# New prices in the plan that orders a mixer's side work, and a sigmoid's product that waits for its sigmoid

## The chip, the cores and the metric

One core of one Trainium2 chip runs the whole program. The metric is the device time of an execution in microseconds (us), shown as the median of several runs; one further execution was recorded by the profiler.

## The reference, cut to what matters

One layer, for a prompt of 1024 positions and 8 samples of 4 positions (1056 columns). A mixer of three head groups, whose outputs are joined and multiplied with `w_out`, and then an MLP with squared ReLU. Each has an RMS norm before and after, with scales from a conditioning vector.

```python
z = h @ w_in
za, zq, zf, zi, zg, zc = split(z)
ya, v_rows = _chunk_gmlp(za, ...)
yb, S = _hgrn2(zq, zf, zi, zg, lb, gn_g, s0)
yc, buf = _conformer_conv(zc, ...)
x = x + gt1 * rmsnorm(concat([ya, yb, yc]) @ w_out)
x = x + gt2 * rmsnorm(square(relu(h2 @ w_up)) @ w_down)
```

The gMLP group is u times a masked product of position weights (128 by 128) with the layer-normalised v, both after a GELU. The recurrence has 8 heads of 64 by 64; chunk by chunk it carries a state S with decay, gives `o = q S + scores v`, normalises o per head and multiplies with `silu(zg)`. The convolution has 31 taps, a layer norm and `y * sigmoid(y)` behind it.

## The kernel before, in words

Everything is kept with features on the partitions and the 1056 columns along the free axis, in three chunks of 352 columns. A **block** is one product of a 1024 by 128 weight with the normalised input: three chunks, 8 slices of the inner dimension, and three matmuls for each slice (`hi*hi`, `lo*hi`, `hi*lo`, both operands being split into two fp32r parts), so 72 matmuls. The results (`pmt`, three banks) are emptied by ScalarE (ACT) and VectorE (DVE). Weights come by DMA as `raw` and are split there as well: ACT writes `whi`, DVE `wlo`.

The blocks of the mixer run in the order convolution 0 and 1, pair 0, gate 0, pair 1, gate 1, pair 2, pair 3, gate 2, gMLP (four blocks: two of v, two of u), gate 3. A pair of heads has three blocks (f, q, v), a gate one, whose product with its sigmoid is `gq`. Behind gate 3, `finish()` lets all side work run to its end, and the output product begins (line 1529; input groups in the order 6, 7, 2, 3, 4, 0, 1, 5, where 6 and 7 are the convolution's, 0 and 1 the gMLP's, and 5 is pair 3).

All other work is side work, written as generators that stand in queues of different rank: `turn` (turned copies of v and k by PE), `recur` (a pair's recurrence), `stage` (its scans and decays), `norm` and `last` (the head norm), `gmlp`, `conv`. Within and after each chunk's products the kernel calls `step(t)` (line 224), which lets the generators go on in order of rank for as long as credit is left on the engines. All engines work in the order in which the program writes, so this decides what stands behind what.

Two things steer it. Each instruction passes through `Metered` (line 85; the instruction itself is issued at line 113), which takes its price from `dve_price`, `ActPrice`, `pool_price` or `pe_price`, charges it to the engine's credit and enters it in a `Plan`, a clock for each engine. And `until(...)` (line 244) makes a generator yield as long as the plan's clock says that the tiles named are not done, or no bank is free. All prices are fixed numbers in the code.

Names that matter below. In a pair's recurrence (`recur`): scores `sc`, sums of states `us`, two scans over the states (DVE), two turned copies `sv` of them by ACT (tiles `vf` and `K` in the trace, 64x960), the output products `ob`, and for the samples `uss` and `os_`, with the state `s0t`. Then `head_norm`: means `gnps` on PE, square root on ACT, three reciprocals on DVE, and the products `k<-k,vf` and `k<-k,gq`. In `stage`: three scans `R` and one over the whole of f. In `conv_tail`: a scale by feature on ACT, the sigmoid on ACT and the product with it on DVE. In `gmlp`: the turned v (`gvt`), its statistics and normalisation on DVE, then `gmps` (four groups of eight matmuls) and `gmsp` on PE, with `gmt` and `gu` behind them on DVE. `split_y` writes the output product's operands `yh` (ACT) and `yl` (DVE).

Of the kernel before, what the change touches and what calls it, by code (L numbers as in the profile page):

```python
# [38 lines left out]
class Plan:  # L39


    def __init__(self):
        self.free = dict.fromkeys(("pe", "act", "dve", "pool", "dma"), 0.0)
        self.done, self.used, self.banks = {}, {}, []
        self.moved = False
# [39 lines left out]
class Metered:  # L85
# [5 lines left out]
    def __getattr__(self, op):  # L91
        f = getattr(self._eng, op)
        if op == "memset":
            return f

        def call(**kw):
            out = kw["out"]
            n = 1
            for x in out.shape[1:]:
                n *= x  # L100
            ins = [x for k, x in kw.items() if k != "out" and hasattr(x, "tensor")]
            if op == "dma_start":
                if self._key == "pool":
                    self._plan.given("pool", 0.9, out, ins, 8.0)
                else:
                    self._plan.given("dma", out.shape[0] * n * 4 / 3e5, out, ins, 2.0)
                return f(**kw)
            price = self._price(op, n, kw)
            self._credit[self._key] -= price
            if self._key == "pe" and op == "matmul" and kw["lhsT"].dtype == F32R:  # L110
                price = n * 0.443e-3 + 0.005
            self._plan.given(self._key, price, out, ins)
            return f(**kw)  # L113

        return call


def dve_price(op, n, kw):
    if op == "reciprocal":
        return 0.1 + n * 6.25e-3  # L120
    if op in ("tensor_scalar", "tensor_copy"):
        return 0.07 + n * 0.55e-3
    if n <= 64:
        return 0.3
    return 0.11 + n * (1.17e-3 if op == "scalar_tensor_tensor" else 1.04e-3)


class ActPrice:
# [3 lines left out]

    def __init__(self):
        self.table = 0

    def __call__(self, op, n, kw):
        t = self.TABLES.get(kw.get("func"), self.table)
        load = 1.3 if t != self.table else 0.0
        self.table = t
        return load + 0.1 + n * 0.83e-3  # L140


def pool_price(op, n, kw):
# [16 lines left out]
def trunk_kernel(ctx: ExitStack, tc: tile.TileContext, xT, cT, wada0, wada, vec, cst, msk, win, wout, wup,  # L160
                 wdn, s0, sconv, aw, aws, arows, yT, hgp, hgs, cvp, cvs, gvs):
    nc = tc.nc
    ctx.enter_context(tc.manual_schedule())
    credit = {"dve": 0.0, "act": 0.0, "pe": 0.0, "pool": 0.0}
    plan = Plan()
    PE = Metered(nc.tensor, pe_price, credit, "pe", plan)
    ACT = Metered(nc.scalar, ActPrice(), credit, "act", plan)
    DVE = Metered(nc.vector, dve_price, credit, "dve", plan)
    POOL = Metered(nc.gpsimd, pool_price, credit, "pool", plan)
    SP = Metered(nc.sync, None, credit, "dma", plan)  # L170
# [12 lines left out]
    def r(ap):  # L183
        return ap.bitcast(F32R)
# [12 lines left out]
    def e(name):  # L197

        while not room():
            step(T_GROUP / 2)  # L200
        held[0] += 1
        return full(name)
# [4 lines left out]
    def rs(name):  # L207
        return sp.tile([128, 512], F32, tag="rs", name=name)
# [35 lines left out]
    def until(*aps, banks=0):  # L244

        while not plan.ready(aps, banks):
            yield 0.2
# [67 lines left out]
    def split_next(later=False):  # L315
# [12 lines left out]
        else:  # L328
            pool = wpools[n_w[0] % len(wpools)]
            hi = pool.tile(shape, F32, tag="whi", name="whi")  # L330
            lo = pool.tile(shape, F32, tag="wlo", name="wlo")
        ACT.copy(out=r(hi), in_=raw)

# [74 lines left out]
    def ada_copy(first):  # L408
        b, ps = first
        sb = mp.tile([128, 128], F32, tag="adasb", name="adasb")  # L410
        ACT.copy(out=sb, in_=ps)
        return b, sb
# [10 lines left out]
    def ada(q):  # L423
# [20 lines left out]
        sb = e("adasb")  # L444
        ACT.copy(out=sb[:, 0:512], in_=ps)
        yield from until(sb, banks=1)
# [37 lines left out]
    def token_rms(ps):  # L484
        n = ps.shape[0]
        rt = sp.tile([128, 4], F32, tag="rt", name="rt", bufs=3)[0:n, :]
        ACT.activation(out=rt, in_=ps, func=AF.Sqrt, scale=1.0 / 1024, bias=eps[0:n])
        return rt
# [21 lines left out]
    def rstd_from(ps):  # L510
        t = rstd_tile("rstd")
        ACT.activation(out=t, in_=ps, func=AF.Sqrt, scale=1.0 / 1024, bias=eps)
        DVE.reciprocal(out=t, in_=t)
# [9 lines left out]
    def add_square(tot, src, m, eng):  # L523

        sq = tot if m == 0 else rs("sqb")[:, 0:tot.shape[1]]
        ACT.activation(out=sq, in_=src, func=AF.Square)
        while pending:
# [403 lines left out]
    def conv_tail():  # L931
        while not room(3):
            yield 2.0
        sq, hi, lo = [e("y6")], e("cvhi"), e("cvlo")
        for c in range(NCH):
            DVE.tensor_tensor(out=ch(sq[0], c), in0=ch(cva[0], c), in1=ch(cva[1], c), op=ALU.add)
        yield 4.0

        def halves():
            ACT.copy(out=r(hi), in_=sq[0])  # L940
            POOL.tensor_tensor(out=r(lo), in0=sq[0], in1=hi, op=ALU.subtract)

        halves()
        yield from until(hi, lo)
        for c in range(NCH):
            yield from until(banks=1)
            mu = pb.tile([128, CW], F32, tag="b", name="cmu")
            mean_of(mu, mean256, ch(hi, c), ch(lo, c))
            s2 = rs("sq2")[:, 0:CW]
            for j in range(2):  # L950
                DVE.tensor_tensor(out=ch(cva[j], c), in0=ch(cva[j], c), in1=mu, op=ALU.subtract)
                ACT.activation(out=s2 if j else ch(sq[0], c), in_=ch(cva[j], c), func=AF.Square)
            DVE.tensor_tensor(out=ch(sq[0], c), in0=ch(sq[0], c), in1=s2, op=ALU.add)
            yield
        yield 4.0
        halves()
        yield from until(hi, lo, banks=3)
        vv = [pb.tile([128, CW], F32, tag="b", name="cvv") for c in range(NCH)]
        for c in range(NCH):
            mean_of(vv[c], mean256, ch(hi, c), ch(lo, c))  # L960
        drop(2)
        sq.append(e("y7"))
        for c in range(NCH):
            ACT.activation(out=ch(sq[0], c), in_=vv[c], func=AF.Sqrt, bias=eps, scale=1.0)
        yield 2.0
        for c in range(NCH):
            sd = ch(sq[0], c)
            DVE.reciprocal(out=sd, in_=sd)
            yield
            for j in range(2):  # L970
                a = ch(cva[j], c)
                DVE.tensor_tensor(out=a, in0=a, in1=sd, op=ALU.mult)
            yield
        yield 2.0
        for j in range(2):
            z = cva[j]
            ACT.activation(out=z, in_=z, func=AF.Identity, scale=vc(V_LNG + j, 1), bias=vc(V_LNB + j, 1))
            yield
            ACT.activation(out=sq[j], in_=z, func=AF.Sigmoid)
            DVE.tensor_tensor(out=sq[j], in0=sq[j], in1=z, op=ALU.mult)  # L980
            ys[6 + j] = sq[j]
            y_done[6 + j] = NCH
            drop()
            yield
# [212 lines left out]
    def recur(p, st):  # L1197
# [73 lines left out]
        yield  # L1271
        for hh in range(2):
            o = 64 * hh
            ACT.copy(out=sv[hh][o:o + 64, 1:16], in_=S[o:o + 64, :, 0:15].rearrange("p d b -> p b d"))
        ACT.copy(out=hg_o[:, p, :], in_=S[:, :, 15])

# [11 lines left out]
        oo, sq, hi, lo = k2, vf, e("gnhi"), e("gnlo")  # L1288
# [19 lines left out]
        for hh in range(2):  # L1308
# [7 lines left out]
                           op=ALU.mult)  # L1316
# [781 lines left out]
```

## Time and profile before

| what | us |
| --- | --- |
| median of 3 runs | 1248.2 (1248.02 to 1248.28) |
| the profiled execution's own time | 1246.52 |
| its span in the trace | 1244.7 |
| TensorE (PE) busy | 1211.6 (97%) |
| VectorE (DVE) busy | 900.4 (72%) |
| ScalarE (ACT) busy | 532.9 (43%) |
| GpSimd (POOL) busy | 62.9 (5%) |

The mixer with its products takes about the first third of the span; the output product's first matmul starts at 405.22. An engine's busy time is what its instructions take, without its waits; PE's has modelled ends, so that rows overlap. In a timeline a bracket at the end of a row is the idle time of the engine just before it, and what ended it. Tile names are the program's, without their numbers, and L113 is the helper's line, common to nearly all instructions.

### The profile page before, as it was taken

Reading aid. Unit: us, or ns where it says so; the run is one execution under the profiler, and the core shown is the slowest. Engines: PE = TensorE matmul, PEld = TensorE weight load, DVE = VectorE, ACT = ScalarE, POOL = GpSimd, SP = SyncE. Lnnn points to the kernel's source line nnn. Section 1 sums busy time; section 2 is a strip of 40 time slices with the busy share of each in tenths; the row PEclk is TensorE's granted clock in tenths of the full one; section 3 lists DMA queues with packets and bytes.
Section 4 is the critical chain, followed back from the end, with each engine's and each line's share of the span. In section 5 each row is a group of like instructions: output and inputs, shape, how many; then the busy total and the mean of one; then the engine's idle time right before and its main releaser. Section 6 shows DMA issues by size and latency. Waiting matters only on the chain.

```text
span 1244.7 us, 20853 instructions
## 1 busy us (share of the span) xinstructions
PE 1211.6 (97%) x8614; PEld 1168.0 (94%) x8614; DVE 900.4 (72%) x1469; ACT 532.9 (43%) x989; POOL 62.9 (5%) x107
## 2 busy tenths in 40 slices
PE   9999999999899999999999999999999999999995
PEld 7888889999889999899999999999999999999994
DVE  5799989687658768767687667657666766765766
ACT  6513364575754756556423312322332331232543
POOL 1000020212010011010000000000000000000001
PEclk9999999999999999999999999999999999999998
DMA  9559411111111475343201211210211121121218
GB/s 366 172 223 279 163 37 53 44 43 43 56 43 40 135 212 136 127 127 119 79 24 51 69 34 35 68 44 24 69 51 35 52 68 34 35 68 35 110 18 212
DMA packets 48846, 113.22 MB, mean 91 GB/s; under 512 B 10336, under 2 KB 24832, under 8 KB 48624
## 3 DMA queue, kind: packets, MB, share of 16 engines
q1 hardware_dynamic: 44432, 99.22, 23.6%
q0 software_dynamic: 4320, 12.68, 4.4%
q8 instruction: 67, 1.10, 0.4%
q14 instruction: 27, 0.22, 0.1%
HBM read 101.75 MB, written 10.14 MB: 90 GB/s over the span
## 4 chain that ended last, share of the span: by engine, by line
PE 83%; DVE 8%; ACT 6%; issue 1%; DMA 1%; POOL 0%; ACTq 0%; DVEq 0%; POOLq 0%
PE pmt L113 75%; PE adaps L113 2%; PE stps L113 1%; DVE acc L113 1%; PE pmt L744 1%; DMA o<-in_xT 1%; DVE wlo L113 1%; ACT K L113 1%; ACT vf L113 1%; DVE q L113 1%; PE sc L113 1%; ACT whi L113 1%; PE ob L113 0%; DVE o L113 0%; DVE vf L113 0%
## 5 line engine op out<-in xcount | busy, mean ns | idle before, releaser
L113 PE MATMUL pmt<-ah,whi 128*128 128x352 f32 (+2 forms) x744 | 241.5, 325 | 1.1 <-ACT ah L113 0.6
L113 PE MATMUL pmt<-al,whi 128*128 128x352 f32 (+2 forms) x744 | 241.3, 324 | 1.0 <-DVE al L113 1.0
L113 PE MATMUL pmt<-ah,wlo 128*128 128x352 f32 (+2 forms) x744 | 240.2, 323 | 0.0
L113 DVE TENSOR_TENSOR acc<-acc,pmt 128x352 f32<-128x352 f32 (+1 forms) x320 | 157.1, 510 | 81.0 <-PE pmt L113 80.0
L113 DVE TENSOR_TENSOR wlo<-raw,whi 128x1024 fp32r<-128x1024 f32 (+2 forms) x113 | 134.5, 1193 | 46.1 <-ACT whi L113 46.1
L113 ACT CAST whi<-raw 128x1024 fp32r<-128x1024 f32 (+2 forms) x113 | 114.2, 1014 | 97.4 <-PE pmt L113 95.6
L113 PEld LDWEIGHTS pmt<-al,whi 128*128 128x128 f32 x744 | 139.9, 188 | 3.7 <-DVE al L113 1.5
L113 PEld LDWEIGHTS pmt<-ah,whi 128*128 128x128 f32 x744 | 139.7, 188 | 2.9 <-ACT ah L113 1.2
L113 PEld LDWEIGHTS pmt<-ah,wlo 128*128 128x128 f32 x744 | 139.8, 188 | 0.4
L113 ACT COPY acc<-pmt 128x352 f32<-128x352 f32 x63 | 28.3, 451 | 196.8 <-PE pmt L113 161.8
L113 PE MATMUL pmt<-h22hi,wlo 128*128 128x352 f32 x256 | 82.7, 323 | 0.0
L113 PE MATMUL pmt<-h22hi,whi 128*128 128x352 f32 x256 | 82.5, 322 | 0.0
L113 PE MATMUL pmt<-h22lo,whi 128*128 128x352 f32 x256 | 82.3, 322 | 0.0
L113 DVE SCALAR_TENSOR_TENSOR cva<-cvx,vec_t,cva 128x1024 f32<-128x1024 f32 x60 | 77.8, 1296 | 1.2
L113 PE MATMUL pmt<-s,whi 128*128 128x352 f32 x312 | 75.6, 324 | 0.0
L113 ACT ACTIVATE relu<-pmt 128x352 f32<-128x352 f32 x57 | 26.4, 463 | 102.4 <-PE pmt L113 102.4
L113 DVE TENSOR_TENSOR al<-rsq,ah 128x352 fp32r<-128x352 f32 x96 | 49.2, 523 | 14.1 <-ACT ah L113 8.0
L113 PE MATMUL pmt<-h1hi,whi 128*128 128x352 f32 x168 | 55.7, 332 | 2.6 <-DVE gq L113 2.6
L113 PE MATMUL pmt<-h0hi,whi 128*128 128x352 f32 x168 | 55.4, 330 | 0.8 <-DVE gq L113 0.8
L113 PE MATMUL pmt<-h2hi,whi 128*128 128x352 f32 x168 | 56.3, 335 | 0.0
L113 DVE TENSOR_TENSOR rsq<-relu 128x352 f32<-128x352 f32 x45 | 23.5, 523 | 43.0 <-ACT relu L113 41.8
L113 PEld LDWEIGHTS pmt<-s,whi 128*128 128x128 f32 x312 | 54.5, 188 | 0.0
(391 smaller groups left out, 2929.8 us busy)
## 6 DMA issues: line engine op xcount, KB each, us to landing
rawada<-in_wada SPq DMA_DIRECT2D x48, 512.0 KB, 8.4
raw<-in_wup SPq DMA_DIRECT2D x36, 512.0 KB, 3.5
raw<-in_wdn SPq DMA_DIRECT2D x48, 256.0 KB, 3.1
raw<-in_win SPq DMA_DIRECT2D x22, 512.0 KB, 3.6
raw<-in_wout SPq DMA_DIRECT2D x20, 512.0 KB, 3.5
raw<-in_wdn SPq DMA_DIRECT2D x12, 512.0 KB, 3.6
x<-in_xT SPq DMA_DIRECT2D x6, 528.0 KB, 6.4
o<-in_xT POOLq DMA_DIRECT2D x6, 528.0 KB, 7.4
```

Of the source, the lines that this page charges most:

```text
L113: return f(**kw)
L744: nc.tensor.matmul(out=pss[m, c], lhsT=r(w_first[m][i % 2][:, k, :]), rhs=r(h[c][i // 2][:, k, :]), start=k == i == 0, stop=k == 7 and i == 2)
```

## The change

Five edits, four of them to prices: a scan costs 0.05 + 2.2e-3 us per element in place of 0.11 + 1.04e-3; the two turned copies `sv` cost 1.75e-3 per element in place of 0.83e-3; each scale or bias that is given by feature adds 0.1 to an ACT instruction; fills (`memset`) are entered in the plan, where they had no price. The fifth is one line in `conv_tail`: the generator yields until the plan says that the sigmoid is done before it issues the sigmoid's product. The arithmetic is the same; what moves is the order.

```diff
@@ -91,7 +91,14 @@
     def __getattr__(self, op):
         f = getattr(self._eng, op)
         if op == "memset":
-            return f
+            def fill(out, value):
+                n = 1
+                for x in out.shape[1:]:
+                    n *= x
+                self._plan.given(self._key, 0.08 + n * 0.85e-3, out, ())
+                return f(out, value)
+
+            return fill
 
         def call(**kw):
             out = kw["out"]
@@ -118,6 +125,8 @@
 def dve_price(op, n, kw):
     if op == "reciprocal":
         return 0.1 + n * 6.25e-3
+    if op == "tensor_tensor_scan":
+        return 0.05 + n * 2.2e-3
     if op in ("tensor_scalar", "tensor_copy"):
         return 0.07 + n * 0.55e-3
     if n <= 64:
@@ -132,12 +141,16 @@
 
     def __init__(self):
         self.table = 0
+        self.turned = False
 
     def __call__(self, op, n, kw):
         t = self.TABLES.get(kw.get("func"), self.table)
         load = 1.3 if t != self.table else 0.0
         self.table = t
-        return load + 0.1 + n * 0.83e-3
+        by_feature = sum(not isinstance(kw.get(x, 0.0), float) for x in ("scale", "bias"))
+        each = 1.75e-3 if self.turned else 0.83e-3
+        self.turned = False
+        return load + 0.1 + n * each + 0.1 * by_feature
 
 
 def pool_price(op, n, kw):
@@ -164,7 +177,8 @@
     credit = {"dve": 0.0, "act": 0.0, "pe": 0.0, "pool": 0.0}
     plan = Plan()
     PE = Metered(nc.tensor, pe_price, credit, "pe", plan)
-    ACT = Metered(nc.scalar, ActPrice(), credit, "act", plan)
+    act_price = ActPrice()
+    ACT = Metered(nc.scalar, act_price, credit, "act", plan)
     DVE = Metered(nc.vector, dve_price, credit, "dve", plan)
     POOL = Metered(nc.gpsimd, pool_price, credit, "pool", plan)
     SP = Metered(nc.sync, None, credit, "dma", plan)
@@ -977,6 +991,7 @@
             ACT.activation(out=z, in_=z, func=AF.Identity, scale=vc(V_LNG + j, 1), bias=vc(V_LNB + j, 1))
             yield
             ACT.activation(out=sq[j], in_=z, func=AF.Sigmoid)
+            yield from until(sq[j])
             DVE.tensor_tensor(out=sq[j], in0=sq[j], in1=z, op=ALU.mult)
             ys[6 + j] = sq[j]
             y_done[6 + j] = NCH
@@ -1271,6 +1286,7 @@
         yield
         for hh in range(2):
             o = 64 * hh
+            act_price.turned = True
             ACT.copy(out=sv[hh][o:o + 64, 1:16], in_=S[o:o + 64, :, 0:15].rearrange("p d b -> p b d"))
         ACT.copy(out=hg_o[:, p, :], in_=S[:, :, 15])
 
```

How the order moves, at three places. First DVE at the end of the convolution, where the two products `y<-y,cva` (128x1056) take the sigmoid; `gq` empties a bank of PE, `QB` is a product of pair 2's `stage`. Before:

```order
L113 TENSOR_TENSOR wlo<-raw,whi 128x1024
L113 TENSOR_TENSOR cva_714<-cva_714,y_2387 128x352
L113 TENSOR_TENSOR cva_1289<-cva_1289,y_2387 128x352
L113 TENSOR_TENSOR gq<-pmt,sgg 128x352
L113 TENSOR_TENSOR y_2387<-y_2387,cva_714 128x1056
L113 TENSOR_TENSOR y_3029<-y_3029,cva_1289 128x1056
L113 TENSOR_TENSOR gq<-pmt,sgg 128x352
L113 TENSOR_TENSOR QB<-q,f 128x32x16
```

And now:

```order
L120 TENSOR_TENSOR cva_714<-cva_714,y_2407 128x352
L120 TENSOR_TENSOR cva_1301<-cva_1301,y_2407 128x352
L120 TENSOR_TENSOR gq<-pmt,sgg 128x352
L120 TENSOR_TENSOR y_2407<-y_2407,cva_714 128x1056
L120 TENSOR_TENSOR gq<-pmt,sgg 128x352
L120 TENSOR_TENSOR wlo<-raw,whi 128x1024
L120 TENSOR_TENSOR y_2966<-y_2966,cva_1301 128x1056
L120 TENSOR_TENSOR s0t<-s0t,uss 128x512
```

The two products stood next to one another between the first and the second `gq`; now the second and the third `gq` and a weight split stand between.

Second, DVE at the end of the mixer, where the reciprocals of `vf` are pair 3's head norm and `gvt` is the gMLP's normalised v. Before:

```order
L113 TENSOR_SCALAR gvt_3953<-gvt_3953,gmv 128x256 x4
L113 TENSOR_SCALAR gvt_3954<-gvt_3954,gmv 128x256 x4
L113 TENSOR_SCALAR gvts<-gvts,gmv 32x256
L113 TENSOR_TENSOR gvt_3953<-gvt_3953,rows 128x1024 x2
L113 TENSOR_TENSOR gvt_3954<-gvt_3954,rows 128x1024 x2
L113 TENSOR_TENSOR gvts<-gvts,rows 32x256 x2
L113 TENSOR_TENSOR wlo<-raw,whi 128x1024
L113 TENSOR_TENSOR gq<-pmt,sgg 128x352
L113 TENSOR_TENSOR k<-k,gq 128x352
L113 TENSOR_TENSOR yl_4156<-y_2387,yh_4155 128x352
```

Here the reciprocals of pair 3 stand ahead of these rows, before the statistics of `gvt`. And now:

```order
L120 TENSOR_TENSOR gvt_3948<-gvt_3948,rows 128x1024 x2
L120 TENSOR_TENSOR gq<-pmt,sgg 128x352 x2
L120 RECIPROCAL vf<-vf 128x352
L120 TENSOR_TENSOR gq<-pmt,sgg 128x352
L120 RECIPROCAL vf<-vf 128x352 x2
L120 TENSOR_TENSOR k<-k,vf 128x352
...
L120 TENSOR_TENSOR yl_4207<-k,yh_4206 128x352 x2
L120 TENSOR_TENSOR gvt_3949<-gvt_3949,rows 128x1024 x2
L120 TENSOR_TENSOR gvts<-gvts,rows 32x256 x2
L120 TENSOR_TENSOR gmt<-gmps,rows 128x512
L120 TENSOR_TENSOR gu_3632<-gu_3632,gmt 128x512
```

The reciprocals have come behind the first half of `gvt`, and the second half of `gvt` behind them and eleven products.

Third, PE at the same place, gate 3's last products (`h2`) and what follows. Before:

```order
L113 MATMUL gmps<-wT,gvt_3953 64x128 x8
L113 MATMUL pmt<-h2hi,whi 128x352
...
L113 MATMUL pmt<-h2hi,wlo 128x352
L113 MATMUL gmps<-wT,gvt_3954 64x128 x8
L113 MATMUL pmt<-h2hi,whi 128x352
...
L113 MATMUL pmt<-h2hi,wlo 128x352
L113 MATMUL gmsp<-wTs,gvts 64x32 x2
L113 MATMUL pmt<-yh_4155,whi 128x352
```

And now:

```order
L120 MATMUL pmt<-h2hi,whi 128x352
L120 MATMUL pmt<-h2lo,whi 128x352
L120 MATMUL pmt<-h2hi,wlo 128x352
L120 MATMUL gmps<-wT,gvt_3948 64x128 x8
L120 MATMUL gmps<-wT,gvt_3949 64x128 x8
L120 MATMUL gmsp<-wTs,gvts 64x32 x2
L120 MATMUL gmps<-wT,gvt_3948 64x128 x8
L120 MATMUL gmps<-wT,gvt_3949 64x128 x8
L120 MATMUL gmsp<-wTs,gvts 64x32 x2
L120 MATMUL pmt<-yh_4206,whi 128x352
```

The groups of `gmps` stood between the products of gate 3; now all four groups and both `gmsp` stand behind the last of them, ahead of the output product.

## Rows read from the trace of the kernel before

**Rows 1.** The page, busy time, share of the span and instructions of TensorE.
```profile
PE 1211.6 (97%) x8614; PEld 1168.0 (94%) x8614; DVE 900.4 (72%) x1469; ACT 532.9 (43%) x989; POOL 62.9 (5%) x107
```

**Rows 2.** Timeline of PE: start us, us, engine, line, operation, tiles, shape [idle before <-releaser].
```profile
164.30 0.27 PE L113 MATMUL ob<-QB,K 128*64 128x64 f32 x1 [0.61 <-ACT K L113]
...
229.15 0.27 PE L113 MATMUL ob<-QB,K 128*64 128x64 f32 x1 [0.68 <-ACT K L113]
...
297.23 0.27 PE L113 MATMUL ob<-QB,K 128*64 128x64 f32 x1 [0.38 <-ACT K L113]
...
321.76 0.43 PE L113 MATMUL pmt<-h0hi,whi 128*128 128x352 f32 x1 [0.84 <-DVE gq L113]
...
329.02 0.43 PE L113 MATMUL pmt<-h1hi,whi 128*128 128x352 f32 x1 [2.62 <-DVE gq L113]
...
333.19 0.51 PE L113 MATMUL sc<-q,k 64*64 64x64 f32 x10 [0.46 <-ACT QS L113]
...
352.02 0.33 PE L113 MATMUL ob<-k,vf 128*64 128x64 f32 x2 [0.54 <-ACT vf L113]
...
353.86 0.27 PE L113 MATMUL ob<-QB,K 128*64 128x64 f32 x1 [1.52 <-ACT K L113]
```

**Rows 3.** Timeline of PE, end of pair 3, gate 3 and first output product.
```profile
359.20 0.43 PE L113 MATMUL pmt<-h2hi,whi 128*128 128x352 f32 x1
...
388.10 0.32 PE L113 MATMUL pmt<-h0hi,whi 128*128 128x352 f32 x1
...
393.82 0.32 PE L113 MATMUL pmt<-h1hi,whi 128*128 128x352 f32 x1
...
397.04 1.09 PE L113 MATMUL gmps<-wT,gvt 128*64 128x128 f32 x16
...
398.07 0.43 PE L113 MATMUL pmt<-h2hi,whi 128*128 128x352 f32 x1
...
399.22 0.30 PE L113 MATMUL gmsp<-wTs,gvts 32*64 32x32 f32 x4
...
405.22 0.43 PE L113 MATMUL pmt<-yh,whi 128*128 128x352 f32 x1
```

**Rows 4.** Timelines of DVE and ACT, where the eight waits of PE come from.
```profile
325.00 1.26 DVE L113 TENSOR_TENSOR y<-y,cva 128x1056 f32<-128x1056 f32 x1 [3.29 <-ACT y L113]
...
350.07 1.89 ACT L113 COPY vf<-q 64x960 f32<-64x960 f32 x1 [4.05 <-DVE q L113]
```

**Rows 5.** Timeline of DVE, pair 3's end, gMLP and gate 3.
```profile
361.30 0.69 DVE L113 TENSOR_TENSOR s0t<-s0t,uss 128x512 f32<-128x512 f32 x1 [8.36 <-POOL s0t L113]
...
367.70 6.77 DVE L113 RECIPROCAL vf<-vf 128x352 f32<-128x352 f32 x3
...
374.76 0.41 DVE L113 BATCH_NORM_STATS2 gbst<-gvt 128x6 f32<-128x256 f32 x1
...
377.96 1.23 DVE L113 TENSOR_TENSOR wlo<-raw,whi 128x1024 fp32r<-128x1024 f32 x1
...
381.99 2.65 DVE L113 TENSOR_SCALAR gvt<-gvt,gmv 128x256 f32<-128x256 f32 x8
...
384.88 4.86 DVE L113 TENSOR_TENSOR gvt<-gvt,rows 128x1024 f32<-128x1024 f32 x4
...
395.78 0.52 DVE L113 TENSOR_TENSOR yl<-k,yh 128x352 fp32r<-128x352 f32 x1
...
396.22 0.69 DVE L113 TENSOR_TENSOR gmt<-gmps,rows 128x512 f32<-128x512 f32 x1
```

**Rows 6.** Windows: stretch, length, busy per engine, granted clock of TensorE, DMA share, GB/s.
```profile
42.00:44.00 2.00, 2.00 (x9) 2.00 (x9) 1.63 (x5) 0.80 (x2) 0.00 (x0) 0.50 0.03 8
```

**Rows 7.** Timeline of ACT, a table load and what follows.
```profile
381.89 1.28 ACT L113 ACT_TABLE_LOAD   x1
383.19 0.46 ACT L113 ACTIVATE gu<-pmt 128x352 f32<-128x352 f32 x1
```

**Rows 8.** Timeline of DVE, a long weight split.
```profile
276.68 2.63 DVE L113 TENSOR_TENSOR wlo<-raw,whi 128x1024 fp32r<-128x1024 f32 x1 [2.84 <-ACT whi L113]
```

## The prediction

> **What bounds the kernel now.** The page first: TensorE (PE) is busy 97% of the span [rows 1]. Only two things can therefore shorten the run: fewer or cheaper matmuls, or the places where PE stands still. The change adds or removes no matmul, so I read PE's timeline through the mixer, the part that the planner orders, and looked for brackets of idle time.
>
> There are eight that the planner's order can mend [rows 2]: five before the products `ob` of a pair (0.61, 0.68, 0.38, 0.54, 1.52), two before a block's first product of a chunk (0.84, 2.62), one before `sc` (0.46). Their sum is 7.65 us. The ends of matmuls are modelled: 36 of them start 0.159 us apart (393.82 less 388.10) while a row says 0.32 [rows 3], so every idle time may be told about 0.16 too short; 8 x 0.16 = 1.3, and the true sum lies between 7.65 and 9.0.
>
> Next, what is late at those places. At 325.00 VectorE (DVE) has stood 3.29 us before the product of y with its sigmoid, since ScalarE (ACT) still computes the sigmoid [rows 4]; behind it in DVE's queue are the `gq` products that empty PE's banks, which is the 2.62 of rows 2. And at 350.07 the turned copy of the states takes 1.89 us for 64x960 elements [rows 4], where the old price says 0.1 + 960 x 0.83e-3 = 0.9; the planner sends PE on to `ob` while the copies still run. So the change prices what really is mispriced.
>
> **The change, part by part: what it gives.** New prices and the new wait cost no instruction. They only move side work: a dearer copy or scan lets the planner put more of PE's products between it and its reader.
>
> (a) In the new order I counted PE's products between the states' sum `us` and its reader `ob`, at 0.159 us each [rows 3]. Pair 0 had 7.8 us and gets 13.3, pair 1 had 7.8 and gets 12.4, pair 2 10.5, pair 3 11.2. Needed are the copies out of `us`, the scans and two copies of about 1.9 us; where the trace has them, the `ob` came 0.4 to 2 us late. All five `ob` waits go, pair 2's with the least room.
>
> (b) The sigmoid's product: DVE now has the last two `gq` and a weight split (`wlo`) ahead of or between the two products, so the waits of 0.84, 2.62 and 0.46 go.
>
> Together -9.0 (upper end of 7.65 to 9.0, since a wait of this size always hides an issue).
>
> (c) fp32 products stand between fp32r products in PE's order, and each change of kind costs: the six `pmt` from 398.07 to 399.22 take 1.15 us, where six at 0.159 are 0.95, so 0.2 a round trip, 0.1 a change [rows 3]. Counted over PE's whole order there are 149 changes before and 135 now: 14 x 0.1 = -1.4 (0 if they overlap with the waits).
>
> **What it costs: the mixer's end.** Nothing of the old trace shows this, it follows from the order. Dearer scans send pair 3's recurrence, and so its norm, some 30 us further back. Before, DVE did the three reciprocals of pair 3 (6.77 us from 367.70) before it came to gMLP's normalisation of `gvt` (381.99 and 384.88), and had that nearly done soon after PE's first product of gate 3 at 388.10 [rows 3, 5]. Now all of this lies on DVE in gate 3, and worse: the second half of `gvt` stands behind the reciprocals and eleven short products. PE, for its part, has all of `gmps` after gate 3's last product, not between them, and the output projection behind that.
>
> So I ran DVE's queue by hand, in us from PE's start of gate 3 (G = 0). Durations are those of the same instructions in rows 5.
> - Pair 3's `os_` ends at -0.9; before, DVE's `s0t` started 2.1 later (361.30 against 359.20 [rows 3, 5]); with a little more queued on ACT it ends at +2.35.
> - Five pairs of statistics at 0.53 (six took 3.2, from 374.76 to 377.96): +4.9. Square root and reciprocals: +5.2. `wlo` waits for its `whi` on ACT: +7.35.
> - Nine TENSOR_SCALAR (2.65 for eight): +10.25. Half of `gvt` (two of the 4.86 for four): +12.65. By then PE has done its 72 products and 6 of `gnps`, 78 x 0.159 = +12.4, and it can do the first eight `gmps` (1.03, from 397.04 to 398.07): about +13.8. There it stops.
> - Two `gq` 0.9, reciprocal 2.26, `gq` 0.44, two reciprocals 4.5: about +20.75. Eleven short products at 0.44 (395.78 to 396.22): +25.6. The second half of `gvt`, 2.4: **+28.0**. PE goes on here, after an idle time of some 14 us.
> - `gvts` 0.8, four pairs `gmt`/`gu` at 1.4 (0.69 each), two small pairs 0.66, three `yl` 1.3: **+36.4**. The last nine matmuls of the first output tile need these `yl`; the tile is done at about +37.0.
>
> Without a stall PE would be there after 78 x 0.159, four `gmps` groups at 1.03, two `gmsp` at 0.25 and 24 x 0.16: +21.1 (before: 405.22 + 3.8 - 388.10 = 20.9 [rows 3], with `gnps` earlier). Loss **+15.9**. Queued behind: the next `wlo`, which PE needs two matmuls later, +0.85.
>
> The clock after the idle time: at the start of the run, after PE had waited, the granted clock was 0.50 in the window 42 to 44 [rows 6], the lower of the two levels, 1.2 GHz; such a window gives away 1.0 us. I take +1.0, with bounds of 0 (the waiting PE's products are small) and 2 (two such windows).
>
> Sum: -9.0 - 1.4 + 15.9 + 0.85 + 1.0 = **+7.3**. The profiled execution took 1246.5 (span 1244.7 and 1.8 around it), so 1253.9; the median of the three runs shown is 1248.2, 1.7 above it, so **1255.5** for the median.
>
> ACT's part of the chain needs table loads, three of them between the square root of `gmv` and the second `sgg` of gate 3. In the trace the load at 381.89 takes 1.28 and the next activation starts at 383.19, 1.30 later [rows 7]; the sum uses 1.3 each. The Trainium skill (ScalarE: Activation LUTs, "What ACT_TABLE_LOAD costs") says that a switch of sets costs a drain of about 1380 ns beside the load of 1283 ns, 2.66 us in all, and by that the sum would come to 1258.3 instead of 1255.5. Here the trace disagrees: 1.30, not 2.66, lies between the load's start and the next activation.
>
> **The rivals.**
> - *Faster: the tail is short.* The place is DVE's queue between `s0t` and the last `yl`. The gains and the tail cancel (but for 1.85 of clock and `wlo`) where the first output tile ends 8.5 us late instead of 15.9, so DVE's chain must be done by about +29, not +36.4. That takes a DVE that reaches `s0t` well ahead, or reciprocals that find idle time earlier. For it: such a queue is run by hand with 40 entries. Against: each wait in it is for something that itself is late, and durations are measured. With a loss of 5 and 0.85 + 1.0 behind it, 1248.2 - 10.4 + 6.9 = 1244.7; with the tail fully hidden 1237.8. Chance 0.11.
> - *It cancels:* the time stays within 0.2%, 1245.7 to 1250.7. Chance 0.10.
> - *The change doesn't do what it says:* waits stay although the order is different. Pair 2 has the least room, and the prices still hold no slow instruction, such as the `wlo` of 2.63 at 276.68 [rows 8] where another took 1.23 [rows 5]. With 2 to 4 us of the waits left, and the clock at its 2 us, 1258 to 1261. Chance 0.10.
> - *ACT is held at its table loads.* If what row 381.89 shows were only half of a load's hold, three loads would bring the second `sgg` 3 x 1.3 = 3.9 later; DVE comes to its `gq` about 1.1 after it is there now, so 2.8 would be left, and 1255.5 + 2.8 = 1258.3. It decides from 1.1 us on. Chance 0.03. By the Trainium skill's rule (ScalarE: Activation LUTs, "What ACT_TABLE_LOAD costs") this would be the likely case.
> - *The forecast:* waits gone, PE stopped between gate 3's last product and the output projection, a loss of 12 to 18 there: 1251 to 1259. Chance 0.66.
>
> **How the numbers follow.** The likeliest case gives 1255.5. Leaving out some 0.14 below and 0.04 above, the range goes from 1247 (the tail about half as long) to 1262 (waits left over on top of the longer end of the forecast's own case). A measurement of this kernel tells about 0.2% from no change, 2.5 us. Faster: 0.11. Within it: 0.10. Slower: 0.66 + 0.10 + 0.03 = 0.79. For the likeliest case alone, 1251 to 1259.
>
> **What would show it.** Right: in PE's timeline the brackets of rows 2 are gone, except small ones; a single idle time of 10 us or more stands before the second group of `gmps`, released by DVE `gvt`; DVE has no idle time from pair 3's reciprocals to the last `yl`; the granted clock has a slice below 1.00 just after. Each mechanism is wrong by itself: (a) if an `ob` waits over 0.5 us on ACT; (b) if DVE still waits over 1 us for a sigmoid of y; (c) if PE's products in the mixer, waits taken off, are not about 1 us shorter. The forecast falls if PE waits less than 6 us at the end of the mixer.

## The result, and the profile after

The changed kernel takes 1255.95 us in the median of 4 runs (1254.17 to 1256.24), the kernel before 1248.24 beside it. The ratio is 1.0059, its 95% interval 1.0044 to 1.0074: slower by 0.6%, about 7.7 us. The profiled execution took 1254.17, with a span of 1252.4.

The line of the page that answers to [rows 1], and the clock in 40 slices:

```profile
PE 1210.7 (97%) x8614; PEld 1168.1 (93%) x8614; DVE 898.9 (72%) x1469; ACT 531.5 (42%) x988; POOL 63.3 (5%) x107
...
PEclk9999999999997999999999999999999999999998
```

PE has no more work than before; it took longer to get through, and one slice in the first third shows a lower clock. The waits of PE from 140 to 420, the stretch of [rows 2] (engine and tile, what it waited for: us in all, times, longest):

```profile
PE gmps L120 <- DVE gvt L120: 14.1, 1, 14.1
PE cvv L120 <- POOL cvlo L120: 0.6, 1, 0.6
```

The eight waits of [rows 2] are gone. One new small one is there, and one of 14.1 us. PE's timeline from gate 3 on shows where it is; these rows answer to [rows 3]:

```profile
376.98 0.40 PE L120 MATMUL pmt<-h0hi,whi 128*128 128x352 f32 x1
...
389.60 1.09 PE L120 MATMUL gmps<-wT,gvt 128*64 128x128 f32 x16
...
404.77 1.97 PE L120 MATMUL gmps<-wT,gvt 128*64 128x128 f32 x16 [14.08 <-DVE gvt L120]
...
407.03 3.68 PE L120 MATMUL gmps<-wT,gvt 128*64 128x128 f32 x32
...
410.95 0.43 PE L120 MATMUL pmt<-yh,whi 128*128 128x352 f32 x1
...
415.43 0.43 PE L120 MATMUL pmt<-yh,wlo 128*128 128x352 f32 x1
```

Gate 3 begins at 376.98, 11.1 us earlier than before (388.10). The first group of `gmps` follows its last product at 389.60 (the trace counts each of its eight matmuls twice, x16); the next group waits 14.08 for DVE's `gvt`. The first output product then starts at 410.95, 5.7 us later than before (405.22). DVE in the same stretch, against [rows 5]:

```profile
378.01 0.69 DVE L120 TENSOR_TENSOR s0t<-s0t,uss 128x512 f32<-128x512 f32 x1 [6.47 <-POOL s0t L120]
...
386.69 2.47 DVE L120 TENSOR_TENSOR gvt<-gvt,rows 128x1024 f32<-128x1024 f32 x2
...
389.94 2.34 DVE L120 RECIPROCAL vf<-vf 128x352 f32<-128x352 f32 x1
...
392.57 4.55 DVE L120 RECIPROCAL vf<-vf 128x352 f32<-128x352 f32 x2
...
402.15 2.48 DVE L120 TENSOR_TENSOR gvt<-gvt,rows 128x1024 f32<-128x1024 f32 x2
...
409.05 0.69 DVE L120 TENSOR_TENSOR gmt<-gmps,rows 128x512 f32<-128x512 f32 x1 [0.52 <-PE gmps L120]
...
413.29 0.52 DVE L120 TENSOR_TENSOR yl<-k,yh 128x352 fp32r<-128x352 f32 x1
```

The first half of `gvt` is done at 389.1; then come the three reciprocals of pair 3 and the short products; the second half runs from 402.15 to 404.6, and PE goes on at once. From 389.1 to the last `yl` DVE stands still only twice, 0.52 and 0.29 for PE's `gmps`. The windows (columns as in [rows 6]) say why PE was slow to deliver them:

```profile
392.00:396.00 4.00, 0.00 (x0) 0.00 (x0) 4.00 (x4) 0.09 (x1) 0.00 (x0) 0.72 0.00 0
...
404.00:408.00 4.00, 3.23 (x30) 2.86 (x32) 3.84 (x7) 0.48 (x1) 0.52 (x1) 0.50 0.05 12
...
408.00:412.00 4.00, 4.00 (x36) 3.63 (x33) 3.08 (x7) 1.50 (x3) 0.00 (x0) 0.64 0.00 0
```

The granted clock fell to 0.50, the lower of the two levels, after PE had stopped, and was still there when the `gmps` ran: a group took 1.9 us (404.77 to 406.67) where [rows 3] has 1.03, and the last two together 3.6 (407.03 to 410.64). No product of the first output tile then waits for `yl`: DVE is done with the last of them at 413.81, before PE wants it.

A table of how far the changed kernel's PE stands from the one before, in us (later is positive), read at the same product in both traces:

| place | before | after | difference |
| --- | --- | --- | --- |
| a product ahead of the part that the change moves | 141.48 | 140.86 | -0.6 |
| gate 3's first product | 388.10 | 376.98 | -11.1 |
| output, first tile's first product | 405.22 | 410.95 | +5.7 |
| output, second tile's first product | 409.19 | 414.92 | +5.7 |
| output, second tile's third product, the first that needs the next `wlo` | 409.55 | 415.43 | +5.9 |
| last chunk's output tiles, after the sums | 468.38 | 475.91 | +7.5 |
| last products | 1221.39 | 1229.27 | +7.9 |

So 10.5 us were won between 141 and gate 3, 17.0 lost from there to the second output tile, and 1.6 more around 470, which nobody had foreseen. The -0.6 at 141 is no effect of the change: in a second profile of the changed kernel the same product starts at 141.62.

### The profile page after: what moved, and what is told of

The parts are those of the page before. It is cut to its first block, busy times and chain, and to the rows that moved or that the text cites. A ratio compares the mean times of both kernels' runs of the same rounds, so it can differ in the third digit from the quotient of the medians.

```text
span 1252.4 us, 20839 instructions
## 1 busy us (share of the span) xinstructions
PE 1210.7 (97%) x8614; PEld 1168.1 (93%) x8614; DVE 898.9 (72%) x1469; ACT 531.5 (42%) x988; POOL 63.3 (5%) x107
## 4 chain that ended last, share of the span: by engine, by line
PE 67%; DVE 6%; ACT 2%; issue 1%; DMA 1%; POOL 0%; DVEq 0%; ACTq 0%; POOLq 0%
PE pmt L120 65%; DVE acc L120 1%; DMA o<-in_xT 1%; DVE gvt L120 1%; DVE vf L120 1%; PE sc L120 0%; DVE o L120 0%; PE gmps L120 0%; PE stps L120 0%; DVE wlo L120 0%; ACT whi L120 0%; DVE rstd L120 0%; PE ob L120 0%; PE us L120 0%; DVE al L120 0%
```

## The experiments

Each ran on the chip beside the kernel before, five times or more. The table gives the median, the ratio with its interval, and the prices that are in.

| run | what is in | us | ratio to before |
| --- | --- | --- | --- |
| changed kernel again | all | 1254.62 | 1.0052 [1.0039, 1.0065] |
| mended end | all, end of the mixer reordered | 1248.15 | 0.9997 [0.9988, 1.0006] |
| no price by feature | scans, copies, fills, sigmoid | 1243.12 | 0.9959 [0.9947, 0.9971] |
| no sigmoid wait | scans, copies, by feature, fills | 1256.2 | 1.0063 [1.0049, 1.0078] |
| scans | scans | 1243.3 | 0.9955 [0.9943, 0.9967] |
| copies | turned copies | 1254.4 | 1.0046 [1.0033, 1.0059] |
| by feature | by feature | 1252.54 | 1.0037 [1.0023, 1.0051] |
| sigmoid | sigmoid's wait | 1250.32 | 1.0015 [1.0005, 1.0024] |
| PE kept busy | all, and 75 idle matmuls | 1255.84 | 1.0057 [1.0044, 1.0071] |
| scans, copies, mended end | scans, turned copies | 1241.88 | 0.9944 [0.993, 0.9958] |
| scans, by feature | scans, by feature | 1240.38 | 0.9933 [0.9918, 0.9947] |
| scans, by feature, mended end | scans, by feature | 1238.44 | 0.9923 [0.991, 0.9936] |

### The end of the mixer alone

Everything ahead of gate 3 stays as in the changed kernel; pair 3's norm goes behind the gMLP's products, and two of its three reciprocals behind the start of the output product.

```diff
-        for c in range(NCH):
+        for c in range(NCH if p < 3 else 0):
             yield
             DVE.reciprocal(out=ch(rd, c), in_=ch(rd, c))
+        while p == 3 and y_done[0] + y_done[1] < 2 * NCH:
+            yield 0.2
         for c in range(NCH):
             yield
+            if p == 3:
+                while c == 1 and not late[1]:
+                    late[0] = True
+                    yield 0.2
+                DVE.reciprocal(out=ch(rd, c), in_=ch(rd, c))
...
-        while any(queues.values()):
+        while any(q for k, q in queues.items() if k != "last") or not late[0]:
...
+            if c == 0 and m == 0:
+                late[1] = True
```

> The changed kernel with only the end of the mixer mended: pair 3's head norm waits for the gMLP's products, its reciprocals are done chunk by chunk, and those of chunks 1 and 2 are put off until the output product has begun. All before gate 3 is the changed kernel's. Theory (DVE's queue makes PE wait, reciprocals and eleven products of pair 3 ahead of the second half of gvt): from gate 3's start, half of gvt is done at +12.65 as before; then three gq 1.35, five yl 2.2 and the second half of gvt 2.4 make +18.6, so PE's idle time of 14.1 shrinks to about 5; gvts 0.8, gmt and gu 6.3, the first chunk's reciprocal 2.3, two products 0.9 and three yl 1.3 bring the last yl to about +30, where it came at +36.7. 6 to 7 us less than the changed kernel: 1249 to 1250. Rival (the idle time is pair 3's late recurrence itself or the clock, whatever stands in DVE's queue): within 2 us of the changed kernel, 1254 to 1257.

Measured: 1248.15, 7 us less than the changed kernel and 0.9 below what was expected (1249 to 1250). PE's two waits at the end, in its timeline:

```profile
396.21 1.98 PE L120 MATMUL gmps<-wT,gvt 128*64 128x128 f32 x16 [4.46 <-DVE gvt L120]
...
408.18 0.43 PE L120 MATMUL pmt<-yl,whi 128*128 128x352 f32 x1 [2.65 <-DVE yl L120]
```

4.46 and 2.65 have taken the place of 14.08. The recurrence of pair 3 is as late and DVE has as many instructions (1469), and the group of `gmps` takes 1.9 us here as well (396.21 to 398.11, at a granted clock of 0.50), so the 7 us come from none of these: that DVE's queue held PE is shown. What is left over is the work that DVE still has to do between pair 3's sums and the first output tile.

### Which price does it

Without the price by feature:

```diff
-        return load + 0.1 + n * each + 0.1 * by_feature
+        return load + 0.1 + n * each
```

> The change without the price of 0.1 for a scale or bias by feature. In the order pair 3's ob then stand 40 us of PE's work ahead of the output product (20 in the changed kernel, 47 before) and DVE's reciprocals are back among the statistics of gvt, while the first two pairs keep 12.3 and 12.4 us between us and ob and pair 3 has 10.5; pair 2 has only 8.6. Theory (gains from us to ob, loss from DVE's queue behind pair 3): the loss of 16 to 18 is gone, the gains stay but for about 1 us at pair 2: 1248.2 - 7 = 1241, 1239 to 1243. Rival (the dearer scans send pair 3 back, as the prediction had it, so that a price of 0.1 does not matter): about 1255.

Measured: 1243.12, 12 us less than the changed kernel, at the upper edge of the expected range. Three of PE's waits there (the largest, 1.19, stands at the convolution's mean):

```profile
303.57 0.27 PE L120 MATMUL ob<-QB,K 128*64 128x64 f32 x1 [1.01 <-ACT K L120]
...
396.59 0.30 PE L120 MATMUL gmsp<-wTs,gvts 32*64 32x32 f32 x4 [0.54 <-DVE gvts L120]
...
402.66 0.43 PE L120 MATMUL pmt<-yl,whi 128*128 128x352 f32 x1 [0.90 <-DVE yl L120]
```

Pair 2's `ob` waits 1.01, as expected, and the stall of the end has shrunk to 0.54 and 0.90. So the dearer scans don't by themselves send pair 3 far back. The scan's price alone (the other prices as before) says the same:

```diff
+    if op == "tensor_tensor_scan":
+        return 0.05 + n * 2.2e-3
```

> The kernel before with the scan's price alone. us to ob: 9.5, 8.6, 8.6 and 8.4 us (7.6, 7.6, 10.5, 7.6 before), pair 3's ob 36 us of PE's work ahead of the output product, the reciprocals ahead of gvt's normalisation. Theory: the ob waits of pairs 0, 1 and 3 shrink by the 1 to 2 us gained there, pair 2's grows by up to 1.5, no stall at the end: 1241 to 1245. Rival (dearer scans are what makes the stall at the end): above 1252.

Measured: 1243.3, as expected, and no long stall at the end. The way there was not quite the expected one: no `ob` of any pair waits, pair 2's neither, and the two waits for `gq`, 0.84 and 2.62 before, come to a single 0.49, though the new wait for the sigmoid is not in this run; PE's largest wait is a new one of 2.19, for an evacuation by ACT (`gvf`). The turned copies alone:

```diff
+            act_price.turned = True
             ACT.copy(out=sv[hh][o:o + 64, 1:16], in_=S[o:o + 64, :, 0:15].rearrange("p d b -> p b d"))
```

> The kernel before with the turned copies' price alone. us to ob: 12.3, 9.5, 12.4 and 10.3 us, so nearly all ob waits (3.7 us told, up to 4.5) should go; the sigmoid's wait of 2.6 may stay. At the end pair 3's ob stand 33 us ahead of the output product, and the order on DVE has gvt's normalisation in two pieces with five yl between them: a stall there of 3 to 8 us. Theory: 1246 to 1252, with an idle time before gmps released by DVE gvt. Rival (the turned copies' price carries the gain and no loss): 1243 or less.

Measured: 1254.4, slower by 0.46% and 2.4 us beyond the range. The stall at the end came as expected, but pair 2's `ob` waits longer than before (two rows of `ob`, two of the stall, and one of ACT):

```profile
307.65 0.33 PE L119 MATMUL ob<-k,vf 128*64 128x64 f32 x2 [1.56 <-ACT vf L119]
...
309.50 0.37 PE L119 MATMUL ob<-QB,K 128*64 128x64 f32 x1 [1.52 <-ACT K L119]
...
402.98 1.98 PE L119 MATMUL gmps<-wT,gvt 128*64 128x128 f32 x16 [4.21 <-DVE gvt L119]
...
406.36 1.98 PE L119 MATMUL gmps<-wT,gvt 128*64 128x128 f32 x16 [1.41 <-DVE gvt L119]
...
300.46 1.07 ACT L119 COPY q<-us 128x512 f32<-128x512 f32 x2
```

The order gave pair 2 12.4 us of products between `us` and `ob`, more than the 10.5 before, and yet 1.56 and 1.52 are waited. ACT's copies out of `us`, the last row, start 9.3 us after PE has done `us` (at 291.1): ACT stands idle until 295.14, by the trace for a product of DVE, and then a gate's activation, a weight cast, a table load and the convolution's square roots stand ahead. The distance on PE alone does not tell what is in between on another engine; the expectation left that out. The price by feature alone:

```diff
+        by_feature = sum(not isinstance(kw.get(x, 0.0), float) for x in ("scale", "bias"))
...
+        return load + 0.1 + n * 0.83e-3 + 0.1 * by_feature
```

> The kernel before with the price by feature alone. us to ob: 7.6, 10.5, 11.9 and 7.6 us, so the ob waits of pairs 1 and 2 go (0.7 and 0.4) and those of pairs 0 and 3 stay (0.6 and 2.1); pair 3's ob 39 us of PE's work ahead of the output product, gvt's normalisation in one piece ahead of gate 3's gq. Theory (the price by feature does harm only where, with the others, it pushes pair 3's ob to 20 us ahead of the output product): no stall at the end, 1246 to 1249. Rival (it does the harm by itself): 1252 or more.

Measured: 1252.54. The rival's number came, but not by the rival's way: the end costs 1.99, and new waits of 2.10 and 2.13 stand in pair 2's blocks and at the convolution's mean:

```profile
256.42 0.66 PE L119 MATMUL pmt<-h2hi,whi 128*128 128x352 f32 x1 [2.10 <-DVE q L119]
...
289.85 0.43 PE L119 MATMUL cvv<-cvhi,means 128*128 128x352 f32 x1 [2.13 <-ACT y L119]
...
410.68 0.42 PE L119 MATMUL pmt<-yl,whi 128*128 128x352 f32 x1 [1.99 <-DVE yl L119]
```

Four of the change's five parts, taken alone (the price of fills was not), thus read -5.6 (scans), +5.6 (copies), +4.8 (by feature) and, below, +2.4 (sigmoid). Their sum, +7.2, is near the change's +7.7 by chance: scans with by feature give -8.4, where their parts would give -0.8, and all but by feature gives -5.7, where the parts would give +2.4. The parts don't add.

### The sigmoid's wait

Alone, on the kernel before:

```diff
             ACT.activation(out=sq[j], in_=z, func=AF.Sigmoid)
+            yield from until(sq[j])
             DVE.tensor_tensor(out=sq[j], in0=sq[j], in1=z, op=ALU.mult)
```

> The kernel before with the wait for the sigmoid alone. On DVE the two products of y move behind the gq and three products of pair 3's stage; nothing else moves but one turned copy. Theory: PE's waits of 0.84 and 2.62 for gq go; pair 3's scores and ob come up to 1 us later for the 2.5 us of products now behind: 1245 to 1247. Rival (the waits only move to pair 3's ob): 1248 to 1249. The wait for gq would have to stay for the part to be idle: 1248.5.

Measured: 1250.32, slower by 0.15%, outside the 1245 to 1247 of the theory and beyond the rival's 1249. Rows of PE, and the last of DVE:

```profile
321.83 0.43 PE L119 MATMUL pmt<-h0hi,whi 128*128 128x352 f32 x1 [0.73 <-DVE gq L119]
...
354.72 0.47 PE L119 MATMUL ob<-k,vf 128*64 128x64 f32 x2 [5.31 <-ACT vf L119]
...
356.57 0.37 PE L119 MATMUL ob<-QB,K 128*64 128x64 f32 x1 [1.38 <-ACT K L119]
...
335.92 1.26 DVE L119 TENSOR_TENSOR y<-y,cva 128x1056 f32<-128x1056 f32 x1 [2.60 <-ACT y L119]
```

The waits of 0.84 and 2.62 of [rows 2] have become 0.73 and nothing, and pair 3's `ob`, which had waited 0.54 and 1.52, waits 5.31 and 1.38. The last row says how: on DVE the second product of y still waits 2.60 for its sigmoid, since `until` asks the plan's clock and not the chip, and now the masks and scans of pair 3 are behind it. And in the changed kernel, the wait taken out:

> The changed kernel without the wait for the sigmoid: only the two products of y move back on DVE, ahead of the second gq of gate 2. By the changed kernel's trace the second y's sigmoid ends at 319.5, so the second gq would come at about 321.2 in place of 315.1; PE's third bank after it is wanted at about 322. Theory (the other prices have given that bank its time): within 1 us of the changed kernel, 1254 to 1257. Rival (the prediction's point b, the wait for the sigmoid is what takes away 0.84 and 2.62): 1258 or more, with PE idle before a chunk's product and released by DVE gq.

Measured: 1256.2, no different from the changed kernel beyond the intervals. One wait comes back, of 0.42:

```profile
319.13 0.43 PE L120 MATMUL pmt<-h1hi,whi 128*128 128x352 f32 x1 [0.42 <-DVE gq L120]
...
405.78 1.98 PE L120 MATMUL gmps<-wT,gvt 128*64 128x128 f32 x16 [14.07 <-DVE gvt L120]
```

So with the other prices in place the sigmoid's wait takes 0.42 us off PE's waits, not the 3.5 of the two `gq` waits, and no difference in time can be told.

### The clock

> The changed kernel as it is, as the measure for the run beside it. 1254 to 1257, with the clock at its lower level from PE's long wait until the output product has begun.

The changed kernel again: 1254.62. With PE kept busy in its long wait:

```diff
+                if j == 0 and i == 1:
+                    for n in range(75):
+                        nc.tensor.matmul(out=filler, lhsT=r(h[0][0][:, 0, 0:128]), rhs=r(h[0][0][:, 0, :]), start=True,
+                                         stop=True, skip_group_check=True)
```

> The changed kernel with 75 matmuls more, of 128x352 on operands at hand, into a bank that nobody reads, ahead of the second group of gmps: 11.9 us of work for PE inside its wait of 14.1 us, so that only some 2 us of waiting are left. No engine waits for them. Theory (the wait costs once by itself and once more by the clock, which the trace has at 0.50 until 410.6): the clock stays at 1.00, the second group of gmps takes 1.0 instead of 1.9, DVE's two waits for gmps (0.52 and 0.29) go, the output product's first tile ends 0.8 earlier; if the low clock at the sums of 472 (0.57, some 1.6 us lost) is the same cause carried on, that goes too: 0.8 to 2.5 us less than the changed kernel, 1253.5 to 1255. Rival (the clock takes nothing there, since DVE's queue sets the end): within 0.3 us of the changed kernel. Rival (PE's filling delays the gmps): slower than the changed kernel.

Measured: 1255.84, no gain; the first theory missed. PE's rows with the filling, and two windows:

```profile
405.37 1.09 PE L120 MATMUL gmps<-wT,gvt 128*64 128x128 f32 x16 [1.80 <-DVE gvt L120]
...
406.69 3.51 PE L120 MATMUL gmps<-wT,gvt 128*64 128x128 f32 x32
...
472.29 1.54 PE L120 MATMUL stps<-sq,cst_t 128*128 128x352 f32 x2 [3.19 <-DVE sq L120]
...
408.00:412.00 4.00, 4.00 (x38) 3.79 (x35) 3.90 (x8) 1.67 (x3) 0.00 (x0) 0.76 0.02 4
472.00:476.00 4.00, 3.71 (x11) 3.21 (x12) 2.74 (x4) 0.56 (x1) 0.00 (x0) 0.50 0.00 0
```

The wait is 1.80, and the second group of `gmps` has its 1.0 us again. But the filling did not keep the clock up: it fell a little later, and the last two groups take 3.45 (406.69 to 410.14) where two groups of 1.03 would take 2.06. The product that needs the next `wlo` starts at 414.93 against 415.70 in the changed kernel beside it, 0.77 earlier; 0.44 of this is a shorter wait for `wlo` (0.15 against 0.59), and the first output tile is done only 0.33 earlier (414.29 against 414.62). At the sums (`stps`) PE then waits 3.19 where it waited 2.26, and the clock falls to 0.50, while beside it, in the changed kernel's profile, it stays at 1.00 there. The chain to the sums goes through transfers of POOL, first in the run with the filling, then in the changed kernel beside it (the bracket is POOL's idle time; in the second rows a landing ended it):

```profile
449.99 0.91 POOL L114 DMA_DIRECT2D o<-in_xT  x1 [43.19 <-DVE o L120]
...
458.52 0.56 POOL L114 DMA_DIRECT2D x1d<-o  x1 [4.50 <-DMA o<-in_xT]
```

```profile
450.74 0.91 POOL L114 DMA_DIRECT2D o<-in_xT  x1 [43.85 <-DVE o L120]
...
458.60 0.56 POOL L114 DMA_DIRECT2D x1d<-o  x1 [3.82 <-DMA o<-in_xT]
```

The first transfer was issued 0.75 earlier (449.99 against 450.74), and the step that waits for its landing came only 0.08 earlier (458.52 against 458.60). What was won at the output's start was lost there. Whether a transfer lands later because of where it falls among others, or by chance, one profile of each can't settle, and these two profiles differ by the clock at the sums as well. All executions together say this much: the mean granted clock was 0.991 or more in five of the six with the filling, against 0.985 to 0.988 in the five of the changed kernel, and their times are no shorter (1252.59 to 1256.84 against 1253.12 to 1256.02). So a higher clock bought nothing that can be told at the end; the size of its part at the output's start stays open.

### Versions that beat both

Scans and turned copies priced, with the mended end:

> The prices of scans and turned copies alone (no price by feature, none for fills, no wait for the sigmoid), with the end of the mixer mended as in the first experiment. us to ob: 12.3, 12.4, 8.6 and 10.5 us, pair 3's ob 42 us ahead of the output product, gmps between gate 3's products. Theory: pair 2's ob waits 1.0 as in the run without the price by feature, the waits of the end there (0.5, 0.9, 0.6) go: 1 to 2 us less than that run's 1243.1, so 1241 to 1242. Rival (the mended end only moves the wait to the second output tile's wlo): 1243 or more.

Measured: 1241.88, as expected; its interval and that of the run without the price by feature (1243.12) overlap. Scans and by feature priced, with the mended end but without its first wait (pair 3's norm need not come behind the gMLP's products):

> The prices of scans and by feature alone, with pair 3's reciprocals done chunk by chunk and those of chunks 1 and 2 put off until the output product has begun. us to ob: 9.5, 8.6, 11.5 and 9.8 us; pair 3's ob 34 us ahead of the output product. Theory: the ob waits of all four pairs are below 0.5, the end has no stall: 1240 to 1242, as the other mended version (1241.9). Rival (34 us are too few, since DVE's chain from s0t to the last yl took 35 in the changed kernel): a wait of 2 to 4 us before the first tile's last products, 1243 to 1245.

Measured: 1238.44, a ratio of 0.9923 [0.991, 0.9936], below the expected range: the fastest here, 17 us less than the changed kernel. All of PE's waits from 140 to 420:

```profile
PE pmt L119 <- ACT gvf L119: 0.3, 1, 0.3
```

And without the mended end:

> The prices of scans and by feature alone, without the mended end, beside the run that has both (1238.4). In the order all else up to gate 3 is the same; on DVE the three reciprocals of pair 3 stand between the halves of gvt, five yl too, and all gmps stand behind gate 3's products. Theory (a mended end is worth what DVE's queue holds PE for): PE waits 1 to 3 us at the end, before gmps or before the first output tile's last products, and 0.6 for the next wlo: 1239.5 to 1242. Rival (the prices do it all): within 0.5 us of 1238.4.

Measured: 1240.38, in the expected range; by ratio 0.9933 [0.9918, 0.9947], so the two intervals overlap and the mended end's share, 1 to 2 us, is told by its waits rather than by the times:

```profile
392.96 0.30 PE L119 MATMUL gmsp<-wTs,gvts 32*64 32x32 f32 x4 [0.55 <-DVE gvts L119]
...
399.03 0.43 PE L119 MATMUL pmt<-yl,whi 128*128 128x352 f32 x1 [0.87 <-DVE yl L119]
...
401.80 0.43 PE L119 MATMUL pmt<-yh,wlo 128*128 128x352 f32 x1 [0.60 <-DVE wlo L119]
```

0.55, 0.87 and 0.60 are the waits that the mended end has removed.

## Why the prediction was right, point by point

- **The sum.** Forecast +7.3 for the profiled execution and 1255.5 for the median; measured +7.65 and 1255.95. By place, the forecast has -9.0 for the waits ahead of gate 3's first product, -0.4 for the switches there (4 of its 14; the other 10 lie behind) and -0.95 for `gnps` (six products at 0.159), which now stand behind that product: -10.35, and -10.5 was measured. From there to the second output tile it has 15.9, 0.85 and 1.0, +0.95 for `gnps` and -1.0 for the ten switches: 17.7, and 17.0 was measured. The term that was too large is the 0.85 for the next `wlo`: in the table the loss grows by only 0.15 (from 5.73 to 5.88) up to the product that needs it. In the second profile of the changed kernel it grows by 0.72 (414.62 to 415.70, against 409.19 to 409.55), while the loss up to the first tile's end, counted from gate 3, is 1.0 smaller. The 1.6 us at the sums of 472 was in no term, and the -0.6 ahead of 141 neither; the good last digit is luck.
- **Two slips in the working.** PE's path without a stall, 78 x 0.159, four groups, two `gmsp` and 24 x 0.16, adds up to 20.9, not 21.1, so the loss by its own terms is 16.1. And the "little more queued on ACT" came from no row: DVE's product with `s0t` ended at +1.7, not at +2.35.
- **DVE's queue by hand.** Forecast, from gate 3's start: half of `gvt` +12.65, PE goes on at +28.0, last `yl` +36.4. The trace: 389.1 (+12.1), 404.77 (+27.8), 413.8 (+36.8). The mended end shows that this queue was the cause. DVE stood still for 0.81 in it, for the slow `gmps`, where the prediction had no idle time. Its last step did not come as told: it is not the last `yl` that ends the first output tile, since no product waits for one there; PE itself, slow at its low clock, is done with the tile at 414.92 (+37.9; the forecast's +37.0 and 1.0 for the clock make +38.0).
- **The waits go (a).** Right for all five `ob`; none of 0.5 us is left, though a new 0.61 stands at the convolution's mean behind POOL. The dearer scans alone do as much: with them no `ob` waits either.
- **The sigmoid's product (b).** The waits went, but the reason given failed: not the new wait takes them away but the other prices (0.42 us without it), and alone it only moves them on to pair 3.
- **The switches (c).** No run takes them by themselves, so they stay argued. Ahead of gate 3, 9.55 us (10.5 less `gnps`) were won, where the waits that went told 7.65 and a new one 0.61; the 2.5 us left over are more than the 0.4 for the switches and the 1.35 by which the forecast raised the waits.
- **"Dearer scans send pair 3's recurrence back"** was wrong as a cause. Dearer scans alone give 1243.3 with no such stall, and all prices but the one by feature give 1243.1. It needs 0.1 us by feature on top of the other prices to move pair 3's `ob` from 40 to 20 us of PE's work ahead of the output product; by feature alone leaves it at 39, scans with by feature at 34. The forecast did not depend on it, since it read the changed order and not the reason for it.
- **The clock.** +1.0 was taken. That the clock fell and the `gmps` were slower for it is shown (1.9 against 1.03 for a group); what that cost is not. Counted from gate 3's first product, the first output tile is done after 37.9 and 37.0 us in two profiles of the changed kernel and after 36.7 with the filling, where the clock fell too. That a second stretch of low clock could follow at the sums was not thought of.
- **The table loads.** In the chain that mattered:

```profile
382.62 1.28 ACT L120 ACT_TABLE_LOAD   x1
383.92 0.47 ACT L120 ACTIVATE sgg<-pmt 128x352 f32<-128x352 f32 x1
387.16 1.28 ACT L120 ACT_TABLE_LOAD   x1
388.45 0.47 ACT L120 ACTIVATE sgg<-pmt 128x352 f32<-128x352 f32 x1
```

A load starts at 382.62 and the next activation at 383.92, 1.30 later, and again 1.29 at 387.16. So the price from [rows 7] held, and the rival in which ACT is held at its table loads falls with it. The Trainium skill's figure of 2.66 us for a switch (ScalarE: Activation LUTs, "What ACT_TABLE_LOAD costs") is not seen here, and neither is the 1258.3 that the sum would have been by it.
- **The rival that it doesn't do what it says** falls for the waits; the rival of a short tail falls with the 14.08, and the one in which gains and tail cancel with the interval, 1.0044 to 1.0074.

## What to carry to other kernels

A correct price in a planner like this one need not be a gain: it changes the whole order, and a tenth of a microsecond more on the instructions with a scale or bias by feature took the same kernel from 1243 to 1256. Judge such a change by the order that comes out: find the last consumer on the busy engine, list what stands ahead of its producer on the producer's engine, and add up those durations; here that hand sum was right to about half a microsecond. And where a long piece (three reciprocals) stands ahead of a short one that PE needs now, the part that is needed only later can be put off.

## What the runs showed that was not expected

PE's wait for the sums of the output (near 470 in the changed kernel, between 456 and 474 in all) lasts 2.1 to 3.2 us in every profile, and in 9 of the 14 the granted clock falls to 0.50 for some microseconds around its end, in 5 it doesn't. The profile first shown, and the same kernel in another run (PE's row, and the window):

```profile
472.02 1.31 PE L120 MATMUL stps<-sq,cst_t 128*128 128x352 f32 x2 [2.34 <-DVE sq L120]
472.00:476.00 4.00, 3.98 (x13) 3.51 (x14) 2.97 (x3) 0.55 (x1) 0.00 (x0) 0.57 0.00 0
```

```profile
472.12 0.86 PE L120 MATMUL stps<-sq,cst_t 128*128 128x352 f32 x2 [2.26 <-DVE sq L120]
472.00:476.00 4.00, 3.88 (x22) 3.67 (x23) 3.39 (x5) 0.56 (x1) 0.00 (x0) 1.00 0.02 8
```

The same wait within 0.1, the clock 0.57 in one and 1.00 in the other, the first two sums 1.31 against 0.86. In the profile first shown that is the step from +5.9 to +7.5 of the table above, 1.6 us. What decides whether the clock falls there no run shows. Two single profiles of one kernel can differ by that much for this alone, so smaller differences can't be read from one profile of each.
